# A two-layer decoder in one kernel: one M1 unit more ahead of P1 and one fewer between P5 and P6

## The chip, the cores and the metric

The kernel runs on one core of a Trainium2 chip. The metric is the device time of one execution in microseconds, the median of several runs. Engines are named as the profile does: PE is TensorE, DVE VectorE, ACT ScalarE, POOL GpSimd, SP SyncE, which here only issues DMAs.

## The reference

A decoder with 512 tokens, width 1024 and two layers, in float32. The first layer mixes tokens by causal averages over windows, the second by a gated spatial unit. Each layer ends in an MLP with 4096 hidden features, and that is where the change lies:

```python
def sq_relu_mlp(h, w1, w2):
    return jnp.square(jax.nn.relu(h @ w1)) @ w2

for i in range(DEPTH):
    ...
    h = modulate(rmsnorm(x, norm_mix_g[i]), sh1, sc1)
    ...  # mixer of the layer
    x = x + g1[:, None, :] * y
    h = modulate(rmsnorm(x, norm_mlp_g[i]), sh2, sc2)
    x = x + g2[:, None, :] * sq_relu_mlp(h, mlp_w1[i], mlp_w2[i])
return rmsnorm(x, final_g)
```

The shifts, scales and gates come from a conditioning vector through a large matrix (`ada_w`), column by column.

## The kernel before

**Products in halves.** To keep float32 accuracy, each operand of a product is split into a high half (ScalarE copies it into a rounded type, line 176 for weights and 638 for activations) and a low half (VectorE subtracts, lines 177 and 639). `mm3` then does three matmuls for one: low by high (line 187), high by low (188), high by high (190). Tiles `wh` and `wl` hold a weight's halves, and there are five pairs of them.

**Seven products for eight.** Most of the MLP's two matrix products are done by blocks of two by two with seven products in place of eight (Strassen's scheme). `mlp(i, ...)`, i = 0 and 1 for the two layers, cuts the hidden features into four chunks. The first product (with `w1`) is M1, the second (with `w2`) M2.

- An M1 unit, `("s", (c, j, m))`, is product m of half j of chunk c: 24 matmuls of 256 columns into `po`, prepared by `s_prep` and run by `s_run`. For m = 5 and 6 VectorE first adds a second block to the weights in place (line 788), and for m = 4 an accumulating DMA does (line 783, GpSimd's queue). Results are combined in the tiles `g` (lines 828 to 836), and squared there.
- An M2 unit, `("p", (c, m))`, written Pm below, is product m of chunk c: 24 matmuls of 512 columns into two banks `pm`, prepared by `p_prep` and run by `p_run`. It takes two pairs of weight halves. Its left operand is a part of `g` or a sum of parts (tiles `s` and `u`, lines 865 to 877), split into `oh` and `ol`. Results are added to `y` (line 930).
- P1, P5, P6 and P4 share one weight tile, `bt`: loaded for P1 (line 846, SP's queue), and after each of P1, P5 and P6 has been split, an accumulating DMA on GpSimd's queue adds the next block to it (line 850). The other M2 weights have tiles `b`.

**The order.** TensorE runs the list `units` in its order. Chunk 0 of M1 is done in other ways, and P units of chunk c stand among M1 units of chunk c + 1. M1 units come in the order m = 1, 5, 6, 3, 7, 2, 4 for j = 0 and then for j = 1, M2 units in the order 1, 2, 5, 6, 3, 7, 4. `lead` M1 units come ahead of P1, and the numbers in `step` say how many follow each M2 unit. Chunk 0 of the first MLP (`early`) has numbers of its own. While unit n runs, `ahead` picks the units behind it to prepare, as many as five weight pairs hold and at most four units on. The other engines' order is set by a scheduler, from the order in which preparation and running are written. Each engine runs its own queue in order.

Between these, `modulation_late` lays the `ada` columns of the next modulation on VectorE (line 215) at fixed places in the list of units.

Of the kernel before, what the change touches and what calls it, by code (L numbers as in the profile page):

```python
# [81 lines left out]
def decoder_kernel(ctx: ExitStack, tc: tile.TileContext, xtok, vecs, rows, fgrow, ada0, adag, ada1, pool_w, w1s, w1, w1f, w1b, w2, w2e, w_v, w_u, w_o, wsT, lnp, bs, out):  # L82
# [561 lines left out]
    def mlp(i, first, extra, last, ending):  # L644
# [3 lines left out]
        with (  # L648
# [328 lines left out]
            for c in range(3):  # L977

                early = i == 0 and c == 0
                fs = [("s", (c + 1, j, m)) for j in range(2) for m in (ORDER2 if early and j == 0 else ORDER)]  # L980
                lead, step = (3, (0, 3, 2, 2, 2, 2, 0)) if early else (2, (1, 2, 3, 2, 2, 2, 0))
                units += fs[0:lead]
                fs = fs[lead:]
                for m, n in zip(ORDER2, step):
                    units.append(("p", (c, m)))
                    units += fs[0:n]
                    fs = fs[n:]
# [118 lines left out]
    ex += [(59, lambda: spread_cols(mods[0][:, c_g(1, 0) : c_g(1, 0) + KD], "gain0"))]  # L1106
    ex += [(n, modulation(q, get4)) for q, n in enumerate(COLUMNS) if q >= 19]
    mlp(0, first0, ex, gated, ending0)


# [6 lines left out]
    with (  # L1117
# [79 lines left out]
        for dh in range(2):  # L1197
            wo = blocks(w_o[dh])

            early = 6 if dh == 0 else KD  # L1200
# [60 lines left out]
    ex = [x for q in range(8) for x in modulation_late(48 + q, 8 + 5 * q, late_gb if q == 0 else get_gb)]  # L1261
    ex += [(58, lambda: spread_cols(mods[1][:, c_g(1, 0) : c_g(1, 0) + KD], "gain1"))]
    mlp(1, first1, ex, last1, lambda: None)


# [78 lines left out]
```

## Time and profile before

| | |
|---|---|
| median of three runs | 855.63 us (854.56 to 855.83) |
| the profiled execution's own time | 853.81 us |
| its span | 852.1 us |
| TensorE busy | 837.4 us (98%) |
| VectorE busy | 695.8 us (82%) |
| ScalarE busy | 490.9 us (58%) |
| mean granted TensorE clock | 0.993 |
| first MLP's chunks with M2 units | about 109 to 338 us of the span |
| second MLP's | about 570 to 800 us |

A profile shows one execution; all its times count from the span's start. TensorE's matmuls are pipelined, so a matmul's length is more than the distance to the next: where TensorE runs without a wait, starts are what to compare. "Idle before" is the time in which an engine had nothing to run, with the instruction or DMA whose end let it go on.

### The profile page before, as it was taken

The numbers are of one execution on the slowest core, as the hardware profiler recorded it, in microseconds if no ns is written. First come the engines' busy times: TensorE is split into PE (matmuls) and PEld (weight loads), VectorE is DVE, ScalarE is ACT, GpSimd is POOL, SyncE is SP. The second block draws the span as 40 slices with busy tenths as digits, with TensorE's granted clock in tenths as the row PEclk, the third lists the DMA queues.
The fourth block names the chain that finished last, engine by engine and source line by source line (L and its number), as shares of the span: only waits on it lengthen the run. The fifth ranks groups of instructions, "written<-read, shape, count | busy, mean of one in ns | idle before, by whom it ended". The sixth has DMA issues, their size and how long they took to land.

```text
span 852.1 us, 13021 instructions
## 1 busy us (share of the span) xinstructions
PE 837.4 (98%) x5068; PEld 744.6 (87%) x5068; DVE 695.8 (82%) x928; ACT 490.9 (58%) x728; POOL 70.3 (8%) x95
## 2 busy tenths in 40 slices
PE   9999999999999999999999999999999999999996
PEld 7778898998998998888888888999999999999885
DVE  6889798978997998867897865777788888987755
ACT  5286776765756567247233226666766666566521
POOL 3000011010101010000020001010101000111001
PEclk9999999999999999999999999999999999999998
DMA  8969998988888896724745636947888788777302
GB/s 349 418 234 323 357 216 217 288 212 236 211 282 195 274 237 205 272 98 173 256 166 176 218 123 224 320 94 202 208 238 221 207 222 241 182 168 243 125 25 99
DMA packets 44082, 186.53 MB, mean 219 GB/s; under 512 B 4955, under 2 KB 5107, under 8 KB 36726
## 3 DMA queue, kind: packets, MB, share of 16 engines
q1 hardware_dynamic: 35282, 137.72, 43.7%
q0 software_dynamic: 8304, 45.63, 26.7%
q10 hardware_dynamic: 436, 2.37, 0.8%
q8 instruction: 40, 0.66, 0.3%
q14 instruction: 20, 0.16, 0.1%
HBM read 179.39 MB, written 6.30 MB: 218 GB/s over the span
## 4 chain that ended last, share of the span: by engine, by line
PE 87%; DMA 6%; ACT 3%; DVE 2%; issue 1%; SPq 0%; POOLq 0%; POOL 0%; DVEq 0%; ACTq 0%
PE po L187 16%; PE po L188 16%; PE po L190 16%; PE pm L188 12%; PE pm L190 12%; PE pm L187 12%; DMA wh<-in_ada 2%; DMA bt<-in_w 2%; DMA wl<-in_ada 1%; DMA ada<-in_adag 1%; PE po L1182 1%; ACT sq L315 1%; PE px L1062 1%; ACT wh L176 0%; PE po L611 0%
## 5 line engine op out<-in xcount | busy, mean ns | idle before, releaser
L187 PE MATMUL po<-hb,wl 128*128 128x256 f32 (+2 forms) x633 | 187.9, 297 | 2.3 <-ACT g L828 2.1
L188 PE MATMUL po<-hb,wh 128*128 128x256 f32 (+1 forms) x632 | 187.2, 296 | 0.0
L190 PE MATMUL po<-hb,wh 128*128 128x256 f32 (+1 forms) x632 | 187.1, 296 | 0.0
L177 DVE TENSOR_TENSOR wl<-raw,wh 128x1024 fp32r<-128x1024 f32 (+1 forms) x128 | 152.8, 1198 | 39.4 <-ACT wh L176 36.8
L176 ACT ACTIVATE wh<-raw 128x1024 fp32r<-128x1024 f32 (+1 forms) x128 | 131.9, 1038 | 79.6 <-PE pm L190 26.7
L190 PE MATMUL pm<-wh,oh 128*128 128x512 f32 (+1 forms) x375 | 131.1, 367 | 0.0
L187 PE MATMUL pm<-wh,ol 128*128 128x512 f32 x336 | 131.0, 390 | 0.0
L188 PE MATMUL pm<-wl,oh 128*128 128x512 f32 x336 | 131.0, 390 | 0.0
L187 PEld LDWEIGHTS po<-hb,wl 128*128 128x128 f32 x633 | 119.6, 189 | 7.0 <-ACT g L828 2.3
L190 PEld LDWEIGHTS po<-hb,wh 128*128 128x128 f32 x632 | 119.5, 189 | 4.1
L188 PEld LDWEIGHTS po<-hb,wh 128*128 128x128 f32 x632 | 119.4, 189 | 3.9
L190 PEld LDWEIGHTS pm<-wh,oh 128*128 128x128 f32 x375 | 70.4, 188 | 14.7
L187 PE MATMUL po<-as,wl 128*128 128x256 f32 x288 | 79.9, 277 | 0.7 <-DVE wl L177 0.7
L188 PE MATMUL po<-as,wh 128*128 128x256 f32 x288 | 79.6, 277 | 0.0
L190 PE MATMUL po<-as,wh 128*128 128x256 f32 x288 | 79.6, 276 | 0.0
L177 DVE TENSOR_TENSOR wl<-bt,wh 128x1024 fp32r<-128x1024 f32 x48 | 58.4, 1222 | 23.5 <-ACT wh L176 23.5
L215 DVE SCALAR_TENSOR_TENSOR ada<-ada,cb 128x1024 f32<-128x1024 f32 x56 | 68.1, 1219 | 10.4 <-DMA ada<-in_ada 7.8
L187 PEld LDWEIGHTS pm<-wh,ol 128*128 128x128 f32 x336 | 63.1, 188 | 11.9
L188 PEld LDWEIGHTS pm<-wl,oh 128*128 128x128 f32 x336 | 63.1, 188 | 11.7
L176 ACT ACTIVATE wh<-bt 128x1024 fp32r<-128x1024 f32 x48 | 50.3, 1057 | 25.6 <-DMA bt<-in_w 15.9
L187 PEld LDWEIGHTS po<-as,wl 128*128 128x128 f32 x288 | 54.1, 188 | 0.9 <-ACT wh L176 0.9
L188 PEld LDWEIGHTS po<-as,wh 128*128 128x128 f32 x288 | 54.2, 188 | 0.0
(218 smaller groups left out, 1549.9 us busy)
## 6 DMA issues: line engine op xcount, KB each, us to landing
ada<-in_ada SPq DMA_DIRECT2D x72, 512.0 KB, 4.5
raw<-in_w1b SPq DMA_DIRECT2D x48, 512.0 KB, 5.5
b<-in_w SPq DMA_DIRECT2D x18, 1024.0 KB, 6.8
bt<-in_w POOLq DMA_DIRECT2D x18, 1024.0 KB, 8.0
raw<-in_w1b POOLq DMA_DIRECT2D x24, 512.0 KB, 5.7
raw<-in_w2e SPq DMA_DIRECT2D x16, 512.0 KB, 4.3
bt<-in_w SPq DMA_DIRECT2D x6, 1024.0 KB, 9.8
b<-in_w POOLq DMA_DIRECT2D x6, 1024.0 KB, 11.1
```

The costliest lines, as they stand in the source:

```text
L176: A.activation(h[:, c], r[:, c], AF.Copy)
L177: V.tensor_tensor(l[:, c], r[:, c], f32(h[:, c]), ALU.subtract)
L187: T.matmul(o[:, c], wl, mh[:, c], start=first and not c.start, stop=False, **kw)
L188: T.matmul(o, wh, ml, start=False, stop=False, **kw)
L190: T.matmul(o[:, c], wh, mh[:, c], start=False, stop=last and c.stop is None, **kw)
L215: V.scalar_tensor_tensor(r, r, 1.0, cb, ALU.mult, ALU.mult, accum_out=pmv[i, b][:, j : j + 1])
L315: A.activation(j, X(t)[:, c], AF.Square, scale=D**-0.5, accum_out=out)
L1062: T.transpose(px[:, 256 * q + P * r : 256 * q + P * r + P], xs[r][:, P * (k + q) : P * (k + q) + P], ident)
L1182: T.matmul(po[:, tok[t]], vt[t][:, ch, c0 : c0 + P], wb[:, 0, hd], start=True, stop=True)
```

## The change

In all chunks but the first of the first MLP, three M1 units stand ahead of P1 rather than two, and two rather than three between P5 and P6.

```diff
                 early = i == 0 and c == 0
                 fs = [("s", (c + 1, j, m)) for j in range(2) for m in (ORDER2 if early and j == 0 else ORDER)]
-                lead, step = (3, (0, 3, 2, 2, 2, 2, 0)) if early else (2, (1, 2, 3, 2, 2, 2, 0))
+                lead, step = (3, (0, 3, 2, 2, 2, 2, 0)) if early else (3, (1, 2, 2, 2, 2, 2, 0))
                 units += fs[0:lead]
                 fs = fs[lead:]
                 for m, n in zip(ORDER2, step):
```

With s1 to s7 for M1 units of j = 0 and t1 to t7 for those of j = 1, TensorE's order in such a chunk is

```
before: s1 s5    P1 s6 P2 s3 s7 P5 s2 s4 t1 P6 t5 t6 P3 t3 t7 P7 t2 t4 P4
now:    s1 s5 s6 P1 s3 P2 s7 s2 P5 s4 t1    P6 t5 t6 P3 t3 t7 P7 t2 t4 P4
```

The scheduler's order on the other engines follows. On VectorE, in chunk 2 of the first MLP, from the low half for s5 on, there stood before (`bt` is P1's weight, `raw_2312` the block that is summed up for s5 and s6, `raw_2420` its second block, `wl_2607` the low half for s6, `ol_2673` and `s_2784` the left operands of P2 and P5):

```order
L177 TENSOR_TENSOR wl_2529<-raw_2312,wh_2528 128x1024
L215 SCALAR_TENSOR_TENSOR ada_2426,pmv_2532<-ada_2426,cb_101 128x1024
L177 TENSOR_TENSOR wl_2597<-bt_2590,wh_2596 128x1024
L177 TENSOR_TENSOR wl_2601<-bt_2590,wh_2600 128x1024
L930 TENSOR_TENSOR y_1176<-y_1176,pm_1897 128x512
L930 TENSOR_TENSOR y_1176<-y_1176,pm_1898 128x512
L788 TENSOR_TENSOR raw_2312<-raw_2312,raw_2420 128x1024
L639 TENSOR_TENSOR ol_2673<-g_2207,oh_2672 128x1024
L865 TENSOR_TENSOR s_2784<-g_1825,g_2207 128x1024
L177 TENSOR_TENSOR wl_2607<-raw_2312,wh_2606 128x1024
```

And there stands now, at the same place (numbers behind a name are new; `wl_2565` is s6's low half, `wl_2603` and `wl_2607` are P1's, `s_2817` and `ol_2704` the left operands of P5 and P2):

```order
L177 TENSOR_TENSOR wl_2529<-raw_2312,wh_2528 128x1024
L215 SCALAR_TENSOR_TENSOR ada_2426,pmv_2532<-ada_2426,cb_101 128x1024
L788 TENSOR_TENSOR raw_2312<-raw_2312,raw_2420 128x1024
L865 TENSOR_TENSOR s_2817<-g_1825,g_2207 128x1024
L930 TENSOR_TENSOR y_1176<-y_1176,pm_1928 128x512
L177 TENSOR_TENSOR wl_2565<-raw_2312,wh_2564 128x1024
L930 TENSOR_TENSOR y_1176<-y_1176,pm_1929 128x512
L177 TENSOR_TENSOR wl_2603<-bt_2596,wh_2602 128x1024
L177 TENSOR_TENSOR wl_2607<-bt_2596,wh_2606 128x1024
L639 TENSOR_TENSOR ol_2704<-g_2207,oh_2703 128x1024
```

The sum and the low half for s6 moved from behind P1's weights to ahead of them, with P5's left operand and one of the two sums on `y` between.

On GpSimd's queue, in chunk 1 of the first MLP, the accumulating DMAs stood in this order (`bt_1804` twice: for P5, then for P6; `raw_1527` for s4):

```order
L783 DMA raw_1602<-in_w1b 128x1024
L850 DMA bt_1804<-in_w2 128x2048
L783 DMA raw_1527<-in_w1b 128x1024
L850 DMA bt_1804<-in_w2 128x2048
L783 DMA raw_2016<-in_w1b 128x1024
```

Now they stand so, `bt_1810` being the same tile:

```order
L783 DMA raw_1602<-in_w1b 128x1024
L783 DMA raw_1527<-in_w1b 128x1024
L850 DMA bt_1810<-in_w2 128x2048 x2
L783 DMA raw_1967<-in_w1b 128x1024
```

The accumulation for s4 moved ahead of the first one on `bt`; the one for P6 stands behind the same things as before.

## The prediction

> **What bounds the kernel now.** I read the page first, then the list of waits, then a table of stretches, then the order of time at the one place that these left. The page's first part, and of the waits the two of TensorE that lie in the MLPs:
>
> ```profile
> PE 837.4 (98%) x5068; PEld 744.6 (87%) x5068; DVE 695.8 (82%) x928; ACT 490.9 (58%) x728; POOL 70.3 (8%) x95
> ...
> PE po L187 <- ACT g L828: 2.1, 1, 2.1
> ...
> PE po L187 <- DVE wl L177: 0.9, 2, 0.7
> ```
>
> TensorE is busy for 98% of the span, and VectorE, which makes the low halves of the weights, is next. What a reordering can win is therefore the time that TensorE loses, and no more. The stretches from the first chunk of the first MLP to the last matmuls say where that is (columns: length, then busy time of PE, PEld, DVE, ACT, POOL, then the granted clock, DMA share and GB/s):
>
> ```profile
> 127.00:130.00 3.00, 1.15 (x11) 0.95 (x9) 1.20 (x2) 2.29 (x3) 0.00 (x0) 1.00 1.03 273
> 130.00:134.00 4.00, 3.75 (x19) 3.76 (x19) 2.35 (x4) 2.09 (x3) 0.85 (x1) 0.57 1.03 320
> 134.00:265.00 131.00, 131.00 (x877) 120.03 (x876) 113.95 (x132) 84.53 (x117) 11.22 (x13) 1.00 0.87 240
> 271.00:273.00 2.00, 1.28 (x11) 1.07 (x10) 2.00 (x2) 2.00 (x4) 0.67 (x1) 1.00 1.02 213
> 273.00:338.00 65.00, 65.00 (x435) 59.45 (x434) 60.49 (x76) 43.95 (x61) 5.84 (x9) 1.00 0.81 237
> 338.00:378.00 40.00, 40.00 (x186) 33.34 (x185) 29.73 (x50) 13.91 (x23) 2.54 (x3) 1.00 0.49 171
> 378.00:548.00 170.00, 169.84 (x898) 145.54 (x897) 132.87 (x214) 78.27 (x122) 11.68 (x15) 1.00 0.59 206
> 548.00:842.00 294.00, 294.00 (x1934) 268.02 (x1934) 235.46 (x258) 178.86 (x236) 22.91 (x29) 1.00 0.66 182
> ```
>
> There are two holes. The one at 127 to 134 us lies in chunk 0 of the first MLP, which keeps its order. The other, at 271 to 273 us, lies in chunk 2 of the first MLP, between P1 and the M1 unit with m = 6 behind it: a place that the change rewrites. All of the second MLP (548 to 842) has no hole at all. Here are the rows of TensorE at the second hole and at the start of that P1, from the timeline (start, length, instruction, idle time before it and what ended that):
>
> ```profile
> 265.38 0.28 PE L190 MATMUL po<-as,wh 128*128 128x256 f32 x1
> ...
> 265.84 0.39 PE L187 MATMUL pm<-wh,ol 128*128 128x512 f32 x1
> ...
> 271.07 0.40 PE L190 MATMUL pm<-wh,oh 128*128 128x256 f32 x2
> 272.18 0.36 PE L187 MATMUL po<-as,wl 128*128 128x256 f32 x1 [0.72 <-DVE wl L177]
> 272.38 0.28 PE L188 MATMUL po<-as,wh 128*128 128x256 f32 x1
> ```
>
> A matmul of 256 columns takes (265.84 - 265.38) / 4 = 0.115 us from start to start, so an M1 unit of 24 takes about 2.7 us. P1 of chunk 2 should have handed over at 271.07 + 2 x 0.115 = 271.30. The next unit began at 272.18, 0.88 late, and its first matmul took 0.20 in place of 0.115: the hole is worth 0.96 us. P1 itself took 271.30 - 265.84 = 5.46.
>
> Why that unit was late is in the rows of VectorE and ScalarE:
>
> ```profile
> 259.29 1.22 DVE L215 SCALAR_TENSOR_TENSOR ada<-ada,cb 128x1024 f32<-128x1024 f32 x1
> ...
> 263.60 1.22 DVE L177 TENSOR_TENSOR wl<-bt,wh 128x1024 fp32r<-128x1024 f32 x1 [3.09 <-ACT wh L176]
> 265.07 1.23 DVE L177 TENSOR_TENSOR wl<-bt,wh 128x1024 fp32r<-128x1024 f32 x1 [0.25 <-ACT wh L176]
> 266.22 1.28 DVE L930 TENSOR_TENSOR y<-y,pm 128x512 f32<-128x512 f32 x2
> 267.41 1.22 DVE L788 TENSOR_TENSOR raw<-raw 128x1024 f32<-128x1024 f32 x1
> ...
> 270.82 1.22 DVE L177 TENSOR_TENSOR wl<-raw,wh 128x1024 fp32r<-128x1024 f32 x1
> ```
>
> ```profile
> 262.51 1.06 ACT L176 ACTIVATE wh<-bt 128x1024 fp32r<-128x1024 f32 x1 [3.82 <-DMA bt<-in_w]
> ...
> 268.67 1.06 ACT L176 ACTIVATE wh<-raw 128x1024 fp32r<-128x1024 f32 x1 [2.68 <-DVE raw L788]
> ```
>
> P1's weights (bt) landed at about 262.5. VectorE stood idle for 3.09 us on them with the sum for m = 6 (L788) queued behind. So the low half of m = 6 ended at 270.82 + 1.22 = 272.04, and TensorE had waited.
>
> **The change, part by part.** It adds and removes no instruction: each engine runs the same work, and 14 M1 units still stand in each chunk. Three M1 units per chunk move: m = 6 in front of P1, m = 3 in front of P2, m = 2 in front of P5. In TensorE's time P1, P2 and P5 start 2.7 us later, the three M1 units earlier (each passes one M2 unit, 5.46), and P6 and all behind it at the old place.
>
> *m = 6 in chunk 2.* It is now wanted at 265.84, where P1 began. In the new order its sum stands directly behind the ada product, which ended at 259.29 + 1.22 = 260.51. From the start of the sum to the end of the low half took 272.04 - 267.41 = 4.63 with two full operations between; now one full operation and one of the two y sums (0.64) stand there, so 4.0 to 4.6. That gives 264.5 to 265.1, 0.7 to 1.3 us before it is wanted. The 3.09 us in which VectorE idled are what it fills. The hole goes: **-0.96 us**.
>
> *P1 in chunk 2.* What is late next would be P1, which now stands behind m = 6 on both engines. ScalarE is free for bt at about 262.8 (sum's end 261.7, one conversion of 1.06); two conversions end at 263.9 and 264.9. VectorE does the second y sum and then the two low halves, to about 266.4 and 267.5. P1 is now wanted at 265.84 + 2.7 = 268.5: 2.1 us of room where it had 265.84 - 264.82 = 1.02. Cost 0.
>
> *Chunk 1 and the second MLP.* TensorE lost nothing there (131.00 of 131, 294.00 of 294), so there is nothing to win. VectorE is 87% busy in the first stretch and 235.46 / 294 = 80% in the second, with the same work as before. Cost 0.
>
> *P5 to P6, one unit fewer.* The rows of chunk 1 are these (VectorE's low half of P5's second weight, the accumulating DMA on bt that follows it, the low half of P6's first weight, P6's first matmul; last, the page's row on those DMAs):
>
> ```profile
> 206.47 1.22 DVE L177 TENSOR_TENSOR wl<-bt,wh 128x1024 fp32r<-128x1024 f32 x1
> ...
> 207.98 0.86 POOL L850 DMA_DIRECT2D bt<-in_w  x1 [14.46 <-DVE wl L177]
> ...
> 218.28 1.22 DVE L177 TENSOR_TENSOR wl<-bt,wh 128x1024 fp32r<-128x1024 f32 x1
> ...
> 222.16 0.39 PE L187 MATMUL pm<-wh,ol 128*128 128x512 f32 x1
> ...
> bt<-in_w POOLq DMA_DIRECT2D x18, 1024.0 KB, 8.0
> ```
>
> P5's second weight was ready at 207.69, the DMA landed some 8.0 after 207.98, P6's first weight was ready at 219.50, and P6 began at 222.16: room of 2.66. At worst P5's weights are made later by the whole unit by which P5 moves; then 2.7 of 2.66 is used, and TensorE waits under 0.1 us in each of two chunks. At best they are made earlier, since VectorE comes there with less behind it. I take 0, since five pairs of weight buffers let VectorE run ahead of P5, and keep 0 to +0.2. On the POOL queue the accumulation for m = 4 now stands ahead of bt's first one; its issue costs 0.86, and P5 comes 2.7 later. On SP a load for an M1 unit moves ahead of an ada load and a b load; neither is wanted sooner than before. Both 0.
>
> Sum: -0.96 against the profiled execution's 853.81, so 852.85. That execution lies 1.82 below the median of the three runs, 855.63, so the median should go to 855.63 - 0.96 = 854.67. A measurement of this kernel can tell about 0.2% (1.71 us) from no change: the forecast lies within.
>
> **What a new hole would cost.** The hole of chunk 0 has the price:
>
> ```profile
> 127.87 0.28 PE L190 MATMUL po<-as,wh 128*128 128x256 f32 x1
> 130.25 0.38 PE L187 MATMUL po<-hb,wl 128*128 128x256 f32 x1 [2.10 <-ACT g L828]
> ...
> 134.69 0.39 PE L187 MATMUL pm<-wh,ol 128*128 128x512 f32 x1
> ```
>
> TensorE stood still for 130.25 - 127.87 - 0.115 = 2.27 us, and the unit behind it took 134.69 - 130.25 = 4.44 in place of 2.7, at a granted clock of 0.57. Together 4.0 us. The hole of 0.88 left the clock at 1.00.
>
> [...]
>
> **The rivals.**
> - *The gain is given back.* The last chunk's weights (w2e) come by DMA, and if they do not come earlier, TensorE waits there for what it won. For it: ScalarE waits on them already.
>
> ```profile
> ACT wh L176 <- DMA raw<-in_w2e: 7.5, 3, 3.3
> ```
>
>  Against it: their loads are issued when VectorE frees buffers, and VectorE comes out of chunk 2 earlier. At most all 0.96 is lost, and P6's 0.2 with it: 855.6 to 855.8.
> - *m = 6 is late, and the result is slower.* Three M1 units now run in 8.2 us in front of P1, and m = 6 needs two sums and two conversions in a row through VectorE and ScalarE, whose queues run in order. The room is 0.7 to 1.3 us; from a lateness of that size on, TensorE waits in front of P1 in chunk 2, where it ran through before. A hole like that of chunk 0 would cost 4.0: 855.63 - 0.96 + 4.0 = 858.7. For it: the smallest room of the new order. Against it: its second block was issued on SP long before,
>
> ```profile
> 246.50 0.33 SPq L159 DMA_DIRECT2D raw<-in_w1b  x1
> ...
> raw<-in_w1b SPq DMA_DIRECT2D x48, 512.0 KB, 5.5
> ```
>
>  and so lands at about 252, and the first block was already summed for m = 5.
> - *More is won.* Only holes can be won, and there is none other from 134 to 548 beyond 0.16 us. A win over 1.71 would need a cause that the trace does not show.
>
> **How the numbers follow.** Forecast 0.60, given back 0.19, m = 6 late 0.16 (with smaller holes in it), more won 0.05. Time: 854.7, the likeliest. The runs before lay 1.07 below to 0.20 above their median, so the range goes from 853.6, which is 1.07 below the forecast, to 857.2, which takes in the gain given back, P6's 0.2 and a small hole of m = 6, but not the full 4.0. Within 0.2%: 0.60 + 0.19 = 0.79; slower 0.16; faster 0.05.
>
> **What would show it.** In the profile after, no wait of TensorE for a low half around 271 us; m = 6 of chunk 2 starting at about 265.8 and P1 at about 268.5 without a wait; P6 of chunk 1 at 222.2 as before; the second MLP with TensorE busy throughout; a span shorter by about 1 us. It is wrong if a stretch of the second MLP shows idle time, if the granted clock drops anywhere between 134 and 548 us, or if the hole reappears in front of P1.

## The result, and the profile after

| | before | after |
|---|---|---|
| median (six runs each) | 855.25 us (853.51 to 857.06) | 859.5 us (859.13 to 860.4) |
| profiled execution's own time; span | 853.81; 852.1 | 859.99; 858.3 |

The change makes the kernel slower: ratio 1.0051 (95% interval 1.0037 to 1.0065). The forecast was 854.7 us. All medians and ratios below leave out one execution of 1416.62 us, at a granted clock of 0.556, in the run with s2 back and thirteen loads out.

The page's first part and the list of waits of the changed kernel (engine, line, what was waited for; us in total, times, longest):

```profile
PE 842.6 (98%) x5068; PEld 747.9 (87%) x5068; DVE 694.3 (81%) x928; ACT 488.9 (57%) x728; POOL 70.4 (8%) x95
...
PE po L187 <- ACT g L828: 2.8, 2, 1.8
PE po L187 <- DVE wl L177: 1.4, 2, 1.2
...
PE pm L187 <- DVE ql L639: 0.4, 1, 0.4
PE pm L188 <- DVE wl L177: 0.4, 1, 0.4
```

There is no less waiting than before, and it lies elsewhere. Of the 2.8 us for L828, 1.79 are a new hole's, and 0.98 are those of chunk 0, which had 2.10 in the kernel before. The table of stretches, cut at the new places (length, then busy time of PE, PEld, DVE, ACT, POOL, then the granted clock, DMA share and GB/s):

```profile
180.00:195.00 15.00, 13.21 (x89) 12.50 (x88) 12.78 (x14) 10.46 (x17) 2.59 (x3) 0.89 0.85 199
195.00:265.00 70.00, 70.00 (x458) 63.70 (x457) 61.05 (x73) 42.63 (x57) 5.17 (x6) 1.00 0.87 242
271.00:273.00 2.00, 2.00 (x11) 1.66 (x10) 2.00 (x4) 1.55 (x2) 0.00 (x0) 1.00 1.03 166
273.00:300.00 27.00, 27.00 (x179) 24.61 (x178) 20.34 (x28) 13.11 (x18) 0.86 (x1) 1.00 0.79 244
300.00:315.00 15.00, 13.76 (x91) 12.42 (x90) 13.87 (x17) 10.58 (x15) 3.16 (x4) 1.00 0.75 137
315.00:338.00 23.00, 23.00 (x153) 20.96 (x152) 21.75 (x29) 14.68 (x22) 1.61 (x3) 1.00 0.74 260
338.00:350.00 12.00, 11.19 (x48) 8.62 (x47) 10.37 (x17) 6.57 (x11) 0.00 (x0) 1.00 0.65 215
548.00:842.00 294.00, 294.00 (x1934) 268.38 (x1933) 234.57 (x252) 180.38 (x241) 22.30 (x28) 1.00 0.67 183
```

The old hole at 271 to 273 us is gone. Three new ones stand where TensorE ran through before: at 188 us in chunk 1, between s5 and s6; at 309 us in chunk 2, between t5 and t6; and at about 346 us, early in the last stage of the MLP. The second MLP has none.

**The hole in chunk 1.** TensorE (the last matmul of s5, the first of s6), then ScalarE from the high half for s6 on:

```profile
188.00 0.28 PE L190 MATMUL po<-as,wh 128*128 128x256 f32 x1
190.06 0.38 PE L187 MATMUL po<-as,wl 128*128 128x256 f32 x1 [1.79 <-ACT g L828]
```

```profile
184.66 1.06 ACT L176 ACTIVATE wh<-raw 128x1024 fp32r<-128x1024 f32 x1 [2.42 <-DVE raw L788]
185.62 1.06 ACT L933 ACTIVATE y<-pm 128x512 f32<-128x512 f32 x2
186.58 2.00 ACT L176 ACTIVATE wh<-bt 128x1024 fp32r<-128x1024 f32 x2
188.47 1.05 ACT L638 ACTIVATE oh<-g 128x1024 fp32r<-128x1024 f32 x1
189.42 0.59 ACT L828 ACTIVATE g<-po 128x512 f32<-128x512 f32 x1
```

s6 did not wait for its weights, which were complete at 186.97 (VectorE's low half started at 185.75 and took 1.22). It waited for L828 at 189.42. `IN_X` puts m = 1 and m = 6 into one PSUM bank: s6 adds onto what s1 left there, so s1's result must be copied out first. That copy stood in ScalarE's queue behind the two `y` copies, P1's two weight conversions and a left operand. Before, the copy came no sooner, but P1's 5.46 us stood between s5 and s6, and s6 came 4.0 us behind its end (190.78). Its rows before (ScalarE's copy, s6's first matmul):

```profile
190.20 0.58 ACT L828 ACTIVATE g<-po 128x512 f32<-128x512 f32 x1
...
194.75 0.29 PE L187 MATMUL po<-as,wl 128*128 128x256 f32 x1
```

**Chunk 2.** VectorE, then ScalarE. The rows at 280.45 and 279.36 are the split for m = 2, those at 284.47 and 286.74 P5's two low halves, those at 298.72 and 297.62 the first split for P6; the row at 299.93 is the sum for t5, the one at 309.23 the low half for t6:

```profile
276.29 1.28 DVE L930 TENSOR_TENSOR y<-y,pm 128x512 f32<-128x512 f32 x2
280.45 1.23 DVE L177 TENSOR_TENSOR wl<-raw,wh 128x1024 fp32r<-128x1024 f32 x1 [2.88 <-ACT wh L176]
...
284.47 1.22 DVE L177 TENSOR_TENSOR wl<-bt,wh 128x1024 fp32r<-128x1024 f32 x1
...
286.74 1.22 DVE L177 TENSOR_TENSOR wl<-bt,wh 128x1024 fp32r<-128x1024 f32 x1
...
298.72 1.23 DVE L177 TENSOR_TENSOR wl<-bt,wh 128x1024 fp32r<-128x1024 f32 x1 [3.74 <-ACT wh L176]
...
299.93 1.22 DVE L788 TENSOR_TENSOR raw<-raw 128x1024 f32<-128x1024 f32 x1
...
309.23 1.23 DVE L177 TENSOR_TENSOR wl<-raw,wh 128x1024 fp32r<-128x1024 f32 x1 [1.13 <-ACT wh L176]
```

```profile
279.36 1.06 ACT L176 ACTIVATE wh<-raw 128x1024 fp32r<-128x1024 f32 x1 [4.40 <-PE po L190]
...
297.62 1.06 ACT L176 ACTIVATE wh<-bt 128x1024 fp32r<-128x1024 f32 x1 [4.26 <-DMA bt<-in_w]
```

The conversion for m = 2 needs its block, whose load started at 271.57 when the low half for s3 had freed a buffer, and a free pair of weight buffers. Both engines stood at it, VectorE for 2.88 us, with P5's split behind. The issues of that block's load (SP) and of the accumulating DMA for P6 (GpSimd):

```profile
271.57 0.33 SPq L159 DMA_DIRECT2D raw<-in_w1b  x1
```

```profile
288.26 0.86 POOL L850 DMA_DIRECT2D bt<-in_w  x1 [17.82 <-DVE wl L177]
```

Before, VectorE's rows for t5's sum, P6's first weight and t6's low half were these:

```profile
294.41 1.23 DVE L788 TENSOR_TENSOR raw<-raw 128x1024 f32<-128x1024 f32 x1 [0.19 <-DMA raw<-in_w1b]
...
295.62 1.22 DVE L177 TENSOR_TENSOR wl<-bt,wh 128x1024 fp32r<-128x1024 f32 x1
...
304.49 1.23 DVE L177 TENSOR_TENSOR wl<-raw,wh 128x1024 fp32r<-128x1024 f32 x1 [1.13 <-PE pm L190]
```

The accumulation was issued at 288.26 in place of 285.30, and P6's first weight was ready at 299.94 in place of 296.84. Of these 3.0 and 3.1 us, 2.40 were handed on by chunk 1: chunk 2, counted from the first matmul of chunk 1's P4, began at 257.32 in place of 254.92. P6 itself had its first weight 1.06 us ahead and did not wait. What came late is the work behind it. VectorE idled 6.6 us at the two splits (2.88 and 3.74), where before it idled 0.4 us on the same stretch, and t5's sum, which had stood ahead of P6's weights, stood behind the first of them. So t6's low half ended 53.14 us from the chunk's start in place of 50.80, and TensorE, which without the old hole wanted it 0.96 us earlier, waited:

```profile
310.60 0.35 PE L187 MATMUL po<-as,wl 128*128 128x256 f32 x1 [1.24 <-DVE wl L177]
```

The backlog reached the last stage. There TensorE waited again, at 345.81 for a low half and at 347.70 for a left operand.

### The profile page after: what moved, and what is told of

The parts are those of the page before. It is cut to its first block, busy times and chain, and to the rows that moved or that the text cites. A ratio compares the mean times of both kernels' runs of the same rounds, so it can differ in the third digit from the quotient of the medians.

```text
span 858.3 us, 13012 instructions
## 1 busy us (share of the span) xinstructions
PE 842.6 (98%) x5068; PEld 747.9 (87%) x5068; DVE 694.3 (81%) x928; ACT 488.9 (57%) x728; POOL 70.4 (8%) x95
## 4 chain that ended last, share of the span: by engine, by line
PE 78%; DVE 8%; ACT 5%; DMA 5%; issue 3%; POOLq 0%; POOL 0%; DVEq 0%; ACTq 0%
PE po L187 14%; PE po L190 14%; PE po L188 14%; PE pm L187 9%; PE pm L188 9%; PE pm L190 9%; DMA bt<-in_w 5%; DVE wl L177 3%; ACT wh L176 2%; PE po L479 1%; PE pg L431 1%; PE pq L465 1%; DVE y L930 1%; DVE ada L215 1%; PE po L1182 1%
## 5 line engine op out<-in xcount | busy, mean ns | idle before, releaser
L188 PEld LDWEIGHTS pm<-wl,oh 128*128 128x128 f32 x336 | 63.1, 188 | 11.7
```

The costliest lines, as they stand in the source:

```text
L188: T.matmul(o, wh, ml, start=False, stop=False, **kw)
```

## The experiments

Unless said otherwise each is compared with the kernel before in the same comparison. To see where time goes, each profiled execution is cut at the same units: chunk 1 from the first matmul of chunk 0's P4 to that of chunk 1's P4; chunk 2 likewise to its own P4; the last stage from there to the third of its second half. From the lengths in the kernel before, 5.46 us for P1 of chunk 1 (189.29 to 194.75) and 5.46 for the two M1 units ahead of it (183.83 to 189.29, 2.73 for one), a chunk without any wait is estimated at 14 x 2.73 + 7 x 5.46 = 76.4 us. "Copy first" is a change on ScalarE that is explained below, "s2 back" the changed kernel with P5 ahead of m = 2 again.

| first MLP's order and what else differs | ratio (95% interval) | chunk 1 | chunk 2 | last stage |
|---|---|---|---|---|
| before | 1 | 76.55 | 77.55 | 38.12 |
| after | 1.0051 (1.0037 to 1.0065) | 80.13 | 78.20 | 39.50 |
| new in chunk 1 alone | 1.0035 (1.0018 to 1.0052) | 79.03 | 78.31 | 38.10 |
| new in chunk 2 alone | 1.0044 (1.0027 to 1.0062) | 78.32 | 79.24 | 39.50 |
| new in the second MLP alone | 1.0008 (0.9988 to 1.0027) | 77.84 | 78.07 | 38.12 |
| after, copy first | 1.0100 (1.0077 to 1.0123) | 80.73 | 81.88 | 39.59 |
| chunk 2: s6 and s3 moved, s2 not | 1.0022 (1.0003 to 1.0041) | 76.96 | 78.76 | 38.10 |
| chunk 2: s2 moved alone | 1.0068 (1.0043 to 1.0093) | 76.87 | 79.74 | 39.59 |
| after, s2 back behind P5 | 1.0017 (1.0003 to 1.0032) | 79.95 | 77.06 | 38.09 |
| the same, copy first | 1.0076 (1.0053 to 1.0100) | 84.42 | 78.21 | 38.10 |
| before, 11 ada loads out | 0.9984 (0.9964 to 1.0005) | 76.75 | 76.59 | 38.09 |
| after, 11 ada loads out | 1.0071 (1.0044 to 1.0098) | 80.79 | 80.62 | 39.51 |
| s2 back, copy first, 11 out | 1.0032 (1.0014 to 1.0049) | 82.53 | 76.59 | 38.10 |
| before, 13 ada loads out | 0.9963 (0.9951 to 0.9975) | 76.44 | 76.59 | 38.10 |
| s2 back, 13 out | 0.9990 (0.9974 to 1.0007) | 80.57 | 76.59 | 38.09 |
| s2 back, copy first, 13 out | 0.9978 (0.9966 to 0.9989) | 77.57 | 76.59 | 38.10 |

**Where it is lost.** The new numbers in one place at a time:

```diff
-(3, (1, 2, 2, 2, 2, 2, 0))
+(3, (1, 2, 2, 2, 2, 2, 0)) if (i, c) == (0, 1) else (2, (1, 2, 3, 2, 2, 2, 0))
```

and so with (0, 2), and with `i == 1`.

> The new order in chunk 1 of the first MLP alone, the old numbers everywhere else. Theory (bank reuse): m = 1 and m = 6 use one PSUM bank, so the M1 unit m = 6 must wait until ScalarE has copied the result of m = 1 out (L828), and that copy stands in ScalarE's queue behind P1's weight conversions. A hole of about 3.7 us between the units m = 5 and m = 6 at about 188 us (1.95 idle and 1.73 at the lowered clock), with the wait put down to ACT g L828; in time +3.6 us, ratio 1.0042 (1.003 to 1.005). Rival (the loss lies in chunk 2 and in the second MLP, and chunk 1's hole is made good behind it): ratio under 1.002.

> The new order in chunk 2 of the first MLP alone. Theory (P5 behind the block for m = 2): the old hole in front of m = 6 is gone (-0.96), but the M1 unit m = 6 with j = 1 between P6 and P3 waits for its low half (about +1.6 at 309 us), and the last stage of the MLP waits for w2e's low halves (about +1.4 at 345 us): net +2.0 us, ratio 1.0024 (1.001 to 1.004). Rival (what the prediction had: P5 to P6 costs nothing in chunk 2, and those holes come from the lateness that chunk 1 hands on): -0.96 us, ratio 0.9989.

> The new order in the second MLP alone. The prediction's step (cost 0 there, all weights are ready 2 us or more ahead): ratio 1.000 (0.9990 to 1.0010), and no wait of TensorE in the second MLP. Rival (the 1.2 us that the stretch around 553 to 585 us took longer in the changed kernel, with a matmul pitch of 0.118 in place of 0.113 us, belong to the change): ratio 1.0014.

Chunk 1 alone costs 0.35%, as the theory had it, with the wait on L828 (1.44 us idle at 188.33). In its profiled execution the clock stayed at 1.00, though, and the hole made P1 1.8 us later, not 3.7. Chunk 2 alone costs 0.44%, more than the 0.24% expected, with the last stage 1.4 us longer and holes at 310.89 (1.65 us) and at about 346 us, though chunk 1 has the old order; the prediction's -0.96 is out. The two costs add up to 0.28% more than the whole change cost, about as much as the three intervals allow. For the second MLP the interval holds both 1.000 and the rival's 1.0014. Its trace decides: no waits there, and the stretch that was 1.2 us longer in the changed kernel was not longer here.

**Is it the bank?** P1's conversions are put behind the copy on ScalarE ("copy first"), and P1 is prepared only after s1 has been run (by a third edit, which is left out here):

```diff
-                    A.activation(t, po, AF.Copy)
+                    held[m] = A.activation(t, po, AF.Copy)
...
-                w = [split(...) for q in range(2)]
+                with tc.issue_after(held[1].ins) if i == 0 and c and m == 1 else nullcontext(): w = [split(...) for q in range(2)]
```

> The changed kernel, but in chunks 1 and 2 of the first MLP P1's two weight conversions are queued on ScalarE behind the copy of m = 1's result. TensorE's order, the weights for m = 6 and VectorE's work for it stay as they are. Theory (bank reuse): the copy ends at about 188.3 in place of 190.0, and the hole at 188 us is gone or under 0.3 us; 3.4 to 3.7 us less than the changed kernel, ratio to the kernel before 1.0006 to 1.0015, and what is left of it is chunk 2's. Rival (the low half for m = 6 comes late through VectorE, as the prediction had it for a hole there): nothing moves, ratio 1.0051.

Right about the hole and wrong about the time. s6 began at 186.84 without a wait on L828, so it was the bank and not the weights. But the kernel got slower than the change: VectorE now waited 4.83 us for m = 2's split in chunk 1 (0.71 in the changed kernel), and P6 of chunk 1 lost 2.12 us. The block for m = 2 was late at the same place and the hole had hidden it: ScalarE could start on that block at 200.75 here, and at 200.59 in the changed kernel. Chunk 2, where the edit holds too, became 3.7 us longer than in the changed kernel.

**Which part of the change costs chunk 2.** P5 back ahead of m = 2, `(3, (1, 1, 3, 2, 2, 2, 0))`, and the opposite, `(2, (1, 3, 2, 2, 2, 2, 0))`, in chunk 2 alone:

> In chunk 2 of the first MLP alone, the first part of the change without the second: three M1 units ahead of P1 and m = 3 ahead of P2, but P5 still ahead of m = 2; everywhere else the old numbers. Theory (the block for m = 2): the load of that block starts only when m = 3's low half frees a buffer, and moved ahead of P5 it makes VectorE wait, with P5's low halves and so the accumulating DMA for P6 behind it. With P5 back in front, VectorE's wait of 2 to 5 us for that block is gone, P6 of chunk 2 has 2 us of room or more, the holes at about 309 and 345 us are gone, and so is the old one at 271 us: -0.96 us, ratio 0.9989 (0.9975 to 1.0005). Rival (m = 6 ahead of P1 is enough: P1's accumulating DMA is issued 3.0 us later, 269.57 for 266.59, and all of P5 and P6 with it): the holes at 309 and 345 us stay, ratio 1.0024 to 1.0044.

> In chunk 2 of the first MLP alone, the second part of the change without the first: two M1 units ahead of P1 as of old, but m = 2 ahead of P5 (one unit fewer between P5 and P6). Theory (the block for m = 2): VectorE waits 2 us or more for that block ahead of P5's low halves, the accumulating DMA for P6 is issued about 2 us later than 285.30, holes of 1 to 2 us each at about 309 and 345 us, the old hole at 271 us stays: +2.5 us, ratio 1.003 (1.001 to 1.005). Rival (m = 6 ahead of P1 is what delays): ratio 1.000.

This separates them. VectorE at the split for m = 2 and at P6's first in the second run, and TensorE's waits in it:

```profile
283.66 1.23 DVE L177 TENSOR_TENSOR wl<-raw,wh 128x1024 fp32r<-128x1024 f32 x1 [3.10 <-ACT wh L176]
299.15 1.23 DVE L177 TENSOR_TENSOR wl<-bt,wh 128x1024 fp32r<-128x1024 f32 x1 [2.10 <-ACT wh L176]
```

```profile
PE pm L188 <- DVE wl L177: 1.5, 3, 0.8
PE po L187 <- DVE wl L177: 1.3, 2, 1.1
...
PE pm L187 <- DVE ql L639: 0.5, 1, 0.5
```

s2 moved alone has the holes at 309 and 345 us; s6 and s3 moved without s2 have neither, with P6's first weight ready 3.6 us ahead, and the last stage is 38.10 as before. From the chunk's start, t6's low half ended at 54.72 us in the one and at 49.88 in the other (50.80 in the kernel before). So it is m = 2 ahead of P5. The second run cost 0.68%, more than expected and more than the whole change; its executions spread from 857.31 to 866.52 us, and the old hole at 271 us, which should have stayed, was not there. The -0.96 of the first did not come out either. That run has a new hole of 1.6 us ahead of P5:

```profile
277.15 1.23 DVE L215 SCALAR_TENSOR_TENSOR ada<-ada,cb 128x1024 f32<-128x1024 f32 x1 [3.02 <-DMA ada<-in_ada]
```

VectorE waited for an ada block, and the `y` sums that clear P5's banks stood behind it.

**Both places together.** The order with P5 back in all chunks, without and with the copy first:

> The changed kernel with P5 back ahead of m = 2 in all chunks: three M1 units ahead of P1, but as many between P5 and P6 as of old. Theory (two causes, bank reuse in chunk 1 and the block for m = 2 in both chunks): the hole at about 188 us with the wait on L828 stays (1.6 to 3.7 us), VectorE's waits for m = 2's block and for P6's weights between 190 and 222 us are under 1 us in place of 2 to 4, and chunk 2 is as in the run with chunk 2 alone: +0.6 to +2.7 us, ratio 1.0007 to 1.003. Rival (m = 6 ahead of P1 is the whole cause): as the changed kernel, ratio 1.005.

> The same, and in chunks 1 and 2 of the first MLP P1's weight conversions queued on ScalarE behind the copy of m = 1's result. Theory (two causes): both are taken away, no hole of TensorE over 0.5 us from 180 to 345 us, -1 us to the kernel before, ratio 0.999 (0.9975 to 1.0005). Rival (VectorE's pace sets chunk 1, as the run with the copy first and the change's order had it when its hole at 188 us came back as two others): the holes come back between 200 and 222 us, ratio 1.003 or more.

The first came as expected: the hole on L828 is there (2.17 us idle), chunk 2 is 77.06, ratio 1.0017. The second went to the rival. One of TensorE's waits, and VectorE's longest in chunk 1 (its profiled execution is the slowest of six, 864.29 us against a median of 860.88):

```profile
PE pm L187 <- DVE y L930: 6.4, 2, 5.0
```

```profile
204.38 1.23 DVE L215 SCALAR_TENSOR_TENSOR ada<-ada,cb 128x1024 f32<-128x1024 f32 x1 [5.94 <-DMA ada<-in_ada]
```

The hole at 188 us had become one of 5.0 us ahead of P5: VectorE stood at an ada load that was issued at 193.86, one of five transfers issued within 5.5 us (the accumulation on bt among them), and landed 10.4 us later.

**Are the loads to blame?** Ada loads left out, eleven of them, with order and work unchanged:

```diff
-r.append(ada_load(ada1[q], get))
+r.append(kept_ada[0] if 7 < q < 19 else kept_ada.__setitem__(0, ada_load(ada1[q], get)) or kept_ada[0])
```

> The kernel before, with eleven of the ada loads of the first MLP left out (those that fall in its chunks 1 and 2; VectorE does the same products on the last block that was loaded, so the modulation columns are not the real ones). No order changes, 5.5 MB less are loaded. Theory (load bursts: what VectorE waits for in these chunks are loads that take 8 to 10 us because several start at once): VectorE's waits over 0.8 us for ada go and those for bt shrink, the old hole at 271 us with them; -1 to -3 us, ratio 0.9965 to 0.999. Rival (the load of an ada block hides behind other work): ratio 1.000.

> The changed kernel with the same ada loads left out (the modulation columns are not the real ones). Theory (load bursts): with fewer loads in flight the block for m = 2 and the accumulated bt land sooner, VectorE waits under 1.5 us for either, and the holes at about 309 and 345 us go; only the hole at 188 us that bank reuse makes is left (1.6 to 3.7 us): 1 to 3.7 us more than the kernel before with the same loads left out. Rival (what counts is the buffer that m = 2's block has to wait for, not the burst): 4.3 us more, with both holes still there.

> P5 back ahead of m = 2, P1's conversions behind the copy of m = 1's result, and the same ada loads left out (the modulation columns are not the real ones). Theory (bank reuse, the block for m = 2, and load bursts behind both): VectorE's wait of 5.94 us for an ada block goes, and with it the holes of 5.2 and 2.5 us ahead of P5 and P6 in chunk 1; no hole over 0.5 us from 180 to 345 us; time as the kernel before with the same loads left out or up to 1 us less. Rival (the later conversions of P1 are what costs, through the accumulating DMAs on bt): 4 to 6 us more than that kernel.

The kernel before came out near the theory (0.9984, chunk 2 without a hole), but the interval holds the rival's 1.000 too, and a wait of 2.05 us for an ada block stayed in chunk 1. For m = 2 the theory fell. Without these loads the change costs as much or more (861.55 - 854.29 = 7.3 us of medians), and VectorE still waits 3.04 us at m = 2's split and 3.94 at P6's, with the last stage 39.51. So it is the position of m = 2, not how many ada loads are in flight. Part of the 7.3 us is the bank again, this time in chunk 2:

```profile
269.39 0.38 PE L187 MATMUL po<-as,wl 128*128 128x256 f32 x1 [1.67 <-ACT g L828]
```

By its time the third run went to the rival (858.67 - 854.29 = 4.4 us more). Its trace has VectorE waiting 4.89 us in chunk 1 for an ada block, because the block of that place was not among the eleven. So two more were left out (`5 < q < 19`):

> The kernel before with thirteen ada loads of the first MLP left out, now with those that VectorE waits for in chunk 1 (the products are done on the last block that was loaded, so the modulation columns are not the real ones). The baseline for the next two: VectorE's wait of 2 to 2.6 us at about 200 us for an ada block goes, TensorE loses nothing over 0.3 us from 175 to 345 us; ratio 0.997 to 0.9995 by either theory.

> Three M1 units ahead of P1, P5 ahead of m = 2 in all chunks, the same thirteen ada loads left out (the modulation columns are not the real ones). Theory (bank reuse alone sets chunk 1's loss): the hole at about 188 us with the wait on L828 stays (1.6 to 3.7 us), no other over 0.3 us follows in the first MLP: 1.6 to 3.7 us more than the baseline. Rival (VectorE's waits for loads set it): within 0.7 us of the baseline from chunk 1's start to its end.

> The same with P1's weight conversions on ScalarE behind the copy of m = 1's result (the modulation columns are not the real ones). Theory (bank reuse, and behind it the ada block that came late): neither is there, no hole over 0.3 us from 175 to 345 us, time within 0.7 us of the baseline. Rival (P1's conversions, 2 us later, delay P5 and P6 through the accumulating DMAs on bt): holes of 2 to 5 us ahead of P5 and P6 in chunk 1, 3 us or more above the baseline.

The first lies a little below its range, at 0.9963, with no hole left. The pair behind it shows the cause in chunk 1, by its traces. With nothing else to wait for, the hole alone makes chunk 1 80.57 in place of 76.44, 4.1 us (2.23 idle, then a slow unit), and 2.6 us of medians (854.23 - 851.64). The granted clock over s6 in the first of the pair:

```profile
188.40:192.40 4.00, 3.91 (x21) 3.91 (x22) 4.00 (x6) 2.62 (x5) 0.86 (x1) 0.60 1.02 187
```

With the copy first it is 77.57, 1.1 above the baseline, of which 0.87 is one wait ahead of P5. That is more than the 0.7 allowed for the medians (853.43 - 851.64 = 1.8), but none of the rival's 3 us. The medians of the pair alone would not tell the two apart: they differ by 0.8 us, and the intervals of the ratios overlap. ScalarE with the copy first:

```profile
186.49 1.06 ACT L638 ACTIVATE oh<-g 128x1024 fp32r<-128x1024 f32 x1
187.44 0.59 ACT L828 ACTIVATE g<-po 128x512 f32<-128x512 f32 x1
187.91 2.02 ACT L176 ACTIVATE wh<-bt 128x1024 fp32r<-128x1024 f32 x2
```

No order that computes the whole reference was faster than the kernel before. These thirteen ada loads cost it 0.37%; where else they could go wasn't tried.

**The sum.** Chunk 1: the new order's mean (80.13, 79.03) less the old one's (76.55, 78.32, 77.84, 76.96, 76.87) is 79.58 - 77.31 = +2.3. Chunk 2: (78.20, 79.24) less (77.55, 78.31, 78.07), 78.72 - 77.98 = +0.7. The last stage: 39.50 - 38.11 = +1.4. Together +4.4, against 859.5 - 855.25 = 4.25 measured. The split within a chunk is uncertain by about 1 us, since chunk 1 in the old order varies from 76.55 to 78.32 between executions; that the sum comes so near is in part luck.

## Why the prediction was wrong

- **"m = 6 in chunk 2: -0.96."** Right for the weights: s6 began at 268.24 without a wait and P1 at 270.96, and the room of s6's low half was 1.8 us (0.7 to 1.3 expected). But the bank was nearly late here too. The copy of m = 1's result ended at 267.95, 0.3 us ahead:

```profile
267.38 0.57 ACT L828 ACTIVATE g<-po 128x512 f32<-128x512 f32 x1
```

 In three other runs with three M1 units ahead of P1, s6 of chunk 2 waited for it (0.34, 0.22 and 1.67 us). What was won in chunk 2 was lost further on.
- **"P1 in chunk 2 ... 2.1 us of room."** Right for TensorE: the first low half was ready at 268.14, 2.8 us ahead. P1's accumulating DMA went out at 269.57 for 266.59, but 2.40 us of that are chunk 1's: from the chunk's start it is 12.25 us, and 11.7 to 12.3 in three executions with the old order. So the 3.0 us of the rival that blamed this DMA were not the change's.
- **"Chunk 1 and the second MLP. TensorE lost nothing there ..., so there is nothing to win. ... Cost 0."** This step failed, for chunk 1. It looked at what could be won and at VectorE's load, and not at what the moved unit needs besides its weights. m = 6 needs the bank of m = 1, and P1 between the two was what covered ScalarE's copy. I had the mechanism in hand: the hole that I took as a price, with its wait "ACT g L828", is s7 of chunk 0 waiting in the same way for s6's copy. I read its length and not its line. By the prediction's own sign, a lower clock between 134 and 548 us, the hole at 188 us spoke against it (0.89 from 180 to 195 us). For the second MLP the step held: no wait there.
- **"P5 to P6 ... I take 0, since five pairs of weight buffers let VectorE run ahead of P5, and keep 0 to +0.2."** This failed too. I priced P5 as moved by one unit, at worst 2.7 us against 2.66 of room, and looked at P6 alone, which did not wait. The moved unit brought a split of its own into queues that run in order: VectorE stood 2.88 us at it with P5's split behind, then 3.74 us at P6's. The work behind that was late, t6's low half by 2.3 us from the chunk's start, and the last stage took 1.4 us longer. Whether the block's landing or the pair of weight buffers ends that wait last differs between executions, the pair in the changed kernel's and the landing in the one above with s2 moved alone. The runs don't tell the two apart.
- **The rival "m = 6 is late"** had nearly the right time (858.7) by luck, with another cause and place: weights in chunk 2, where the weights' room was good.
- **"What a new hole would cost", 4.0.** Two holes of this size agree: 1.95 + 1.73 = 3.7 at 188 us in the changed kernel (clock 0.71 from 190.00 to 192.50), and 4.1 in the run with s2 back and thirteen loads out. But the clock's share is not given by the idle time. In the second of them 2.23 us of idling were followed by 0.60 (188.40 to 192.40, above). In the run with s2 back behind P5 2.17 us of idling left the clock at 1.00, and the hole cost 2.5 us:

```profile
189.40:192.40 3.00, 2.90 (x24) 2.90 (x25) 3.00 (x4) 2.64 (x5) 0.86 (x1) 1.00 1.02 175
```

 Chunk 0's hole of 2.10 us was followed by 0.57 in the kernel before (130.00 to 134.00), and by 1.00 in the run with chunk 2 alone (130.60 to 133.40). In the first MLP of these sixteen traces, four of the seven holes of 1.78 to 2.23 us were followed by a lowered clock, and none of the eight of 1.42 to 1.70 us was. What makes the difference no run shows. The price of the hole at 188 us was 1.8 to 4.1 us.

## What to carry to other kernels

When a unit is moved ahead, list everything that it waits for, not its weights alone: the PSUM bank that it adds onto, with the engine that must empty it and what stands in that engine's queue, and the unit that used to stand between and hid it (here 1.79 us idle behind the copy, which P1's 5.46 us had covered). Then follow what the moved unit puts in front of others in queues that run in order (here 2.88 and 3.74 us of VectorE), out to the next DMA that is issued only when they are done. With the copy first, the wait that was taken from TensorE came back twice at the next late operand (2.12 us ahead of P6, 5.0 us ahead of P5), so the test of a mechanism is a run in which that next one is gone as well. And count the times of a stage from its own start: most of what seemed late in chunk 2 had been handed on by chunk 1.

## What was not expected of the hardware

A hole of nearly the same idle time was followed by the lowered clock in some executions and not in others (0.60 after 2.23 us, 1.00 after 2.17 us, above). And the first stretch of the second MLP, from f4, the first of the four units in which chunk 0 of M1 is done there, to s1, took either 21.76 or 22.61 us, with no wait in it. It took the longer time in nine of the sixteen profiled executions, with the old order and with the new, so that 0.85 of the 6.2 us by which the two profiled spans differ is not the change's. The same 24 us of it in the changed kernel and in the one before (busy times and matmuls, then clock):

```profile
553.00:577.00 24.00, 24.00 (x206) 24.00 (x205) 16.84 (x15) 14.67 (x20) 1.73 (x2) 1.00 0.52 134
```

```profile
548.00:572.00 24.00, 24.00 (x214) 24.00 (x214) 17.60 (x16) 15.62 (x22) 1.73 (x2) 1.00 0.48 130
```

Both were granted the full clock, and 214 matmuls ran in the one and 206 in the other. The cause stays open.
